# Spreading the weight sums of a down product over two earlier stages, and four small moves in linear attention, in a one-core Trainium2 kernel

## The chip, the cores and the metric

The kernel runs on one core of one Trainium2 chip, as one program. The metric is the time of one execution in microseconds (us) on the device. Before the change three runs took 1881.84, 1878.85 and 1880.43 us, a median of 1880.43 us.

The engines are called as the profile calls them: PE (TensorE, the matmuls; PEld its weight loads), DVE (VectorE), ACT (ScalarE), POOL (GpSimd) and SP (SyncE, which only issues transfers here). POOL issues transfers too, on a queue of its own. Each engine works through its instructions in order, and an instruction that waits holds up all behind it on that engine.

## The reference: what is computed

One step of one layer of a streaming encoder, for two groups of requests together (1024 + 32 rows; the kernel keeps them as 1056 columns, features along the partitions):

```python
h = rms_norm(x, g_pre_mix)
qa, ka, va, ra, alr, qb, kb, vb, ga, gb = split_cols(h @ w_in)
oa, s_gla = gla_branch(qa, ka, va, ra, alr, w_a2, b_a2, g_gla, gla_s0, gla_block)
ob, k_rows, v_rows = attn_fn(qb, kb, vb, rel_bias)
mix = (jax.nn.sigmoid(ga) * (oa @ w_br_a) + jax.nn.sigmoid(gb) * (ob @ w_br_b)) @ w_out
x = x + rms_norm(mix, g_post_mix)
f, conv_new = conv_ffn(rms_norm(x, g_pre_ffn), conv_s0, w_up, conv_w, conv_b, w_down)
x = x + rms_norm(f, g_post_ffn)
gate = jax.nn.sigmoid(rms_norm(x, g_pre_ple) @ w_ple_gate)
x = x + rms_norm(gate * (pe @ w_ple), g_post_ple)
```

`gla_branch` is linear attention with a gate (4 heads, in blocks of rows, with a state carried from block to block), `attn_fn` is softmax attention in a band (8 heads), and `conv_ffn` is an up product (1024 to 2 x 2816), a short causal convolution, a gelu and a down product (2816 to 1024). All of it is float32.

## The kernel before, in words

**Products.** Every fp32 weight is split into a high half `whi` (a copy by ACT) and a low half `wlo` (weight minus high half, by DVE); inputs likewise. A product is then three matmuls: high by high, high by low, low by high. The large products use a Strassen-Winograd scheme: of the eight quarter products of a 2 x 2 partition only seven are formed, from sums of the quarters of the weight and of the input. So weight sums have to be made before such a product begins.

**Stages**, in us from the start of the profiled execution: norm and preparations (0 to 80), the first part of the in product (to 290), attention in a band (to about 560), linear attention (564 to 860), the branch products (to 980), the out product (to 1075), part of the up product ahead of its sums (to 1170), the rest of the up product (to 1540), the down product (to 1770), and the last gate with its norm (to 1875.9). The matmuls that are left of the in product, for the merge gates `ga` and `gb`, are filler: `piece` (L900) issues one small piece of them, and both attentions call it wherever PE would else wait.

**The gate tiles.** A piece on a tile called `Item` ends, after two pieces, in a tile `fv`, written by two ACT copies (L867) from PSUM, and `into` (L745) stores this tile to its places in DRAM (`d_ga`, `d_gb`). Some places are written plainly, others are added to. There are 56 such tiles and 72 stores, 32 plain and 40 that accumulate. All 72 go out on POOL's queue (L748). There are four buffers of `fv`. A tile's weights are split ahead: the high half by ACT (L814, L817), and the low half by DVE (L815, L818), which is put on a list, `fill["lows"]`, that the next `piece` carries out (`lows`, L794). Evacuations of PSUM are put on a list too, `fill["done"]`, and are carried out by `flush` or, all but the last, by `tidy`.

**Weight sums for the down product.** `weight_sum(i, m, at)` (L1152) makes one of sixteen sums of quarters of `w_down`, in DRAM, with three transfers on POOL's queue. It writes one element of its destination `d_ws[i, m]` from a tile that was just computed (L1154; here called the marker, which ties the sum to this place in the program); it copies one quarter there, 704 KB from DRAM to DRAM (L1155); and it adds the second quarter with an accumulating transfer (L1132). The last step goes through the list `later` in `second_sum`, and comes two sums later. The copy waits for the marker, the accumulating transfer for the copy. `branch_sum` (L1134, markers L1138, copies L1139) does the same for the branch product's weights, in sixteen smaller sums of 256 KB each into `d_wa`, during the band. The sums with i = 1 and 3 take `d_ws[0]` and `d_ws[1]` as their first term. The sixteen calls of `weight_sum` stand in `up_strassen(f)` (L2587), one in each f from 0 to 15; f = 16 and 17 call the last two accumulating transfers.

**The band.** Its loop (L1263 on) has nine steps j for each of eight heads g, two heads to a pair hp. `prepare` of the next head fills parts of its tile `bias` on POOL (L976, L977). `band_sums` fills `sums` on POOL (L1162). `branch_sum` stands at j = 1, 4 and 7 of the heads from g = 1 on. VectorE's row sums come at L1035 to L1042.

**Linear attention.** It has sixteen units u = (head h, block s). Each forms scores at several levels: products in PSUM (`one`), copied under masks by DVE into `scores` (`score_copies`, L1470 to L1478), turned by PE (`score_turn`, L1444) and copied back by ACT (`turned`, L1445). Exponentials for the next unit run on ACT (L1364 to L1377). The roots for the norm are L1561 to L1566. `gate_sigmoid` (L834, L835) takes the sigmoids of four gate tiles during u = 15, in two halves each. `slot` (L1652) issues filler pieces; `turn_back` is handed to `level_products` and runs in the middle of the unit. After MAIN pieces the filler is the band's branch product (L890), whose evacuation multiplies by the gates (L844).

**The up product.** `up_strassen(f)` runs for f = 0 to 21. It loads two weight tiles on SP's queue, `raw` and `sraw` (L2497), forms weight sums `ws` on DVE (L2504), and multiplies (L2521 to L2523). For sixteen of the f, the list AHEAD, two of the seven products were made before and stand in DRAM (`d_e`), from where `p1` (L2531) and the first half of `av` (L2582) are loaded on SP's queue. L2580 adds the product of `s2` into the second half of `av`, L2586 forms `q`, whose first element is the marker of the weight sum, and outputs go from `av` and `sm` to `d_b` on POOL's queue (L2364). `av` has three buffers, `sm` one, `raw` and `sraw` two each.

**What sets the order.** In most stages the order on PE, DVE and ACT is the order of the code (a manual schedule); the order on POOL and SP, and on every engine in `up_strassen`, is set by a list scheduler when the program is built.

Of the kernel before, what the change touches and what calls it, by code (L numbers as in the profile page):

```python
# [114 lines left out]
def emit(tc, a):  # L115
# [629 lines left out]
    def into(acc, *places):  # L745
        def store(t):
            for d, h in places:
                po.dma_start(d[:, h], t, **({"accum_op": ALU.add} if acc else {}))  # L748
        return store

    class Item:
# [40 lines left out]
    def lows():  # L792
        for f in fill["lows"]:
            f()  # L794
        fill["lows"].clear()
# [43 lines left out]
    def gate_sigmoid(n):  # L839
        sigmoid(GB[n], GB[n], n)  # L840
# [56 lines left out]
                    yield  # L897
        yield

    def piece():  # L900
        if fill["now"] is None:
            if fill["at"] == len(units):
                return
            fill["now"] = unit_parts(*units[fill["at"]]), 0
        tidy()
        lows()
        parts, n = fill["now"]
        next(parts)
        i, c = units[fill["at"]]
        item = isinstance(tiles[i], Item)  # L910
        fill["now"] = (parts, n + 1) if n < 2 and not item else None
        if n == 0 and fill["split"] == i + 1 <= FIRST and (c in (0, 2) if item else c < 2):
            split_half(int(c > 0))
            if c:
                fill["lows"].append(load_tile)
        if fill["now"] is None:
            fill["at"] += 1
        fill["n"] += 1
        if fill["n"] in PLACES:
            place(*PLACES[fill["n"]])  # L920
# [336 lines left out]
    for i in range(len(WORK) + SK + 1):  # L1257
        g, j = divmod(i, NW)
        hp, hd = divmod(g, 2)
        if g < 8:  # L1260
            if j == 0:
                if hd == 0:
                    band_sums(hp)  # L1263
                steps = prepare(g + 1) if g < 7 else decays(0)
            if j == 3 and hd == 0:
                B[hp]["ob"] = evt()
            WORK[i][0]()
            if SK <= i:
                WORK[i - SK][1]()
            B[hp]["exp"].pop()()  # L1270
            next(steps, None)
            if j % 3 == 2:
                next(made, None)
            if hd == 0 and hp < 3 and j in (5, 7) or hd and hp < 3 and j == 0:
                band_row(hp + 1, {5: 0, 7: 1, 0: 2}[j])
            if g == 7 and j in (6, 7):
                head_value(0, j - 6)
            if j % 3 == 1 and g:
                n = 3 * (g - 1) + j // 3
                if n < 4 * HK:  # L1280
                    branch_sum(n, B[hp]["sums"][hd][0:1, 0:1])
# [317 lines left out]
    flush()  # L1599
    differences(0, range(1, 6))  # L1600
    piece()
    exponentials(0, (7, 6))
    flush()
    piece()
    exponentials(0, (1, 2, 3))
# [43 lines left out]

    SKIP = (5, 8)  # L1650

    def slot(k=1):  # L1652
        for i in range(k):
            slots[0] += 1
            if OB.get("h") is not None or fill["n"] < MAIN and slots[0] % 9 not in SKIP:
                piece()

    level_start(0)
    for u in range(16):
# [29 lines left out]
        def turn_back():  # L1689
            if u == 15:  # L1690
                slot(2)
            if u:
                output_turns(u - 1)
            slot(1)

        level_products(u, (states, turn_back))
        flush()
        if u < 15:
            exponentials(u + 1, (1, 2, 3, 4))
            flush()  # L1700
        score_copies(u, range(4, 7))
        slot(1)
        score_turn(u)
# [8 lines left out]
            results(u - 1)  # L1712
        if u == 15:
            gates(u)
            gate_sigmoid(2)
            gate_sigmoid(3)
            branch_split(1)
        if u < 15:
            factors(u + 1, (7,))
# [44 lines left out]
                OB[x] = tl(bo, [P, 4, T], F32R, tag="b" + x)  # L1764
        if u == 15:
            log_exp()
        roots(u)
        if u == 14:
            branch_split(0)
# [724 lines left out]
    def up_strassen(f):  # L2494
# [89 lines left out]
        Z_ = Z[:, :, :HC]  # L2584
        mul(Z, weight(s1, WL_ENG[2]), "t1", True, True)
        ve.tensor_tensor(q, p1, Z_, op=ALU.add)  # L2586
        if f < 16:  # L2587
            weight_sum(*divmod(f, 4), q[0:1, 0, 0:1])
        elif f < 18:
            second_sum()  # L2590
        if not ahead:
            mul(X, weight(a12, WL_ENG[3]), "b21", False, True)
# [705 lines left out]
```

## Time and profile before

| | |
|---|---|
| median of three runs | 1880.43 us (1878.85 to 1881.84) |
| the profiled execution's own time | 1877.64 us |
| its span in the trace | 1875.9 us |
| mean granted clock of TensorE | 0.994 of full speed |
| busy: ACT, POOL | 1004.4 us (54%), 370.7 us (20%) |
| DMA, POOL's own queue | 161.90 MB, 33.7% of 16 engines' span |
| DMA, SP's and the other hardware queues' | 244.34 MB, 39.2% |
| bytes moved by all queues | 413.24 MB, mean 220 GB/s |

The profile is of one execution, and its span is 1.7 us less than that execution's own time. Busy times count matmuls, copies and the like, on POOL also the issue of transfers. A row of the waits names the waiting group (engine, tile, line), what released it, and then the total us, the number of waits and the longest. In a timeline a row has its start, its duration, the engine and line, and in brackets the idle time before it and what ended it; SPq is SP's queue. The "granted clock" is the share of full speed that TensorE was given.

### The profile page before, as it was taken

The numbers are of one execution on the slowest core, as the hardware profiler recorded it, in microseconds if no ns is written. First come the engines' busy times: TensorE is split into PE (matmuls) and PEld (weight loads), VectorE is DVE, ScalarE is ACT, GpSimd is POOL, SyncE is SP. The second block draws the span as 40 slices with busy tenths as digits, with TensorE's granted clock in tenths as the row PEclk, the third lists the DMA queues.
The fourth block names the chain that finished last, engine by engine and source line by source line (L and its number), as shares of the span: only waits on it lengthen the run. The fifth ranks groups of instructions, "written<-read, shape, count | busy, mean of one in ns | idle before, by whom it ended". The sixth has DMA issues, their size and how long they took to land.

```text
span 1875.9 us, 36253 instructions
## 1 busy us (share of the span) xinstructions
PE 1828.2 (97%) x14000; PEld 1790.9 (95%) x14000; DVE 1298.5 (69%) x2451; ACT 1004.4 (54%) x2126; POOL 370.7 (20%) x641
## 2 busy tenths in 40 slices
PE   9999999999999999999999999999999999999997
PEld 8999998999998998999999999999998999999996
DVE  6955543666656777787756867888876875558776
ACT  7544234666667687675545555333332345555555
POOL 0043341131102231110000121222233211000112
PEclk9999999999999999999999999999999999999999
DMA  7278987567537899887584576789898679987746
GB/s 289 78 230 239 274 215 231 155 189 196 143 113 252 249 255 253 207 222 262 157 272 157 169 274 258 236 249 284 241 250 235 164 204 306 279 285 244 235 150 111
DMA packets 169402, 413.24 MB, mean 220 GB/s; under 512 B 21956, under 2 KB 56972, under 8 KB 168332
## 3 DMA queue, kind: packets, MB, share of 16 engines
q1 hardware_dynamic: 111548, 244.34, 39.2%
q0 software_dynamic: 56240, 161.90, 33.7%
q10 hardware_dynamic: 1440, 4.69, 0.6%
q8 instruction: 110, 1.80, 0.4%
q14 instruction: 64, 0.52, 0.1%
HBM read 270.68 MB, written 181.97 MB: 241 GB/s over the span
## 4 chain that ended last, share of the span: by engine, by line
PE 78%; DMA 6%; DVE 6%; ACT 5%; issue 4%; POOL 1%; SPq 0%; DVEq 0%; ACTq 0%; POOLq 0%
PE two L2521 5%; PE two L2523 5%; PE two L2522 5%; PE two L641 4%; PE two L642 4%; PE two L643 4%; PE two L2970 3%; PE mm L228 3%; PE mm L226 3%; PE two L2972 3%; PE two L2971 3%; PE mm L227 3%; PE mm L890 3%; PE mm L892 2%; PE mm L891 2%
## 5 line engine op out<-in xcount | busy, mean ns | idle before, releaser
L2972 PE MATMUL two<-d,wlo 128*128 128x264 f32 x616 | 174.3, 283 | 0.8 <-DVE wlo L2706 0.8
L2971 PE MATMUL two<-d,whi 128*128 128x264 f32 x616 | 174.7, 284 | 0.2 <-DVE d L2657 0.2
L2970 PE MATMUL two<-d,whi 128*128 128x264 f32 x616 | 174.6, 284 | 0.0
L859 PE MATMUL mm<-xh,whi 128*128 128x264 f32 x448 | 135.2, 302 | 3.6 <-ACT fv L867 3.5
L2511 ACT ACTIVATE whi<-ws 128x512 fp32r<-128x512 f32 x88 | 55.5, 632 | 155.1 <-PE two L2522 147.0
L860 PE MATMUL mm<-xl,whi 128*128 128x264 f32 x448 | 127.4, 284 | 0.0
L861 PE MATMUL mm<-xh,wlo 128*128 128x264 f32 x448 | 127.2, 284 | 0.0
L2522 PE MATMUL two<-ml,whi 128*128 128x264 f32 x448 | 126.5, 283 | 0.0
L2523 PE MATMUL two<-mh,wlo 128*128 128x264 f32 x448 | 126.0, 284 | 0.0
L2521 PE MATMUL two<-mh,whi 128*128 128x264 f32 x448 | 125.8, 283 | 0.0
L2972 PEld LDWEIGHTS two<-d,wlo 128*128 128x128 f32 x616 | 116.4, 189 | 1.1 <-DVE wlo L2706 1.0
L2971 PEld LDWEIGHTS two<-d,whi 128*128 128x128 f32 x616 | 115.8, 188 | 0.4 <-DVE d L2657 0.4
L2970 PEld LDWEIGHTS two<-d,whi 128*128 128x128 f32 x616 | 115.7, 188 | 0.0
L890 PE MATMUL mm<-xh,whi 128*128 128x352 f32 x312 | 108.6, 348 | 1.0 <-ACT fv L734 1.0
L892 PE MATMUL mm<-xh,wlo 128*128 128x352 f32 x312 | 100.9, 324 | 0.0
L891 PE MATMUL mm<-xl,whi 128*128 128x352 f32 x312 | 100.7, 323 | 0.0
L642 PE MATMUL two<-tl,whi 128*128 128x264 f32 x320 | 90.7, 284 | 0.0
L641 PE MATMUL two<-th,whi 128*128 128x264 f32 x320 | 90.7, 284 | 0.0
L643 PE MATMUL two<-th,wlo 128*128 128x264 f32 x320 | 90.7, 284 | 0.0
L859 PEld LDWEIGHTS mm<-xh,whi 128*128 128x128 f32 x448 | 85.0, 190 | 5.5 <-ACT fv L867 4.9
L2706 DVE TENSOR_TENSOR wlo<-wraw,whi 128x512 fp32r<-128x512 f32 (+1 forms) x81 | 51.7, 643 | 49.7 <-ACT whi L2705 49.5
L860 PEld LDWEIGHTS mm<-xl,whi 128*128 128x128 f32 x448 | 84.6, 189 | 0.0
(801 smaller groups left out, 6891.0 us busy)
## 6 DMA issues: line engine op xcount, KB each, us to landing
raw<-in_w_in SPq DMA_DIRECT2D x36, 512.0 KB, 4.8
d_b<-av POOLq DMA_DIRECT2D x33, 528.0 KB, 8.0
d_ws<-in_w_down POOLq DMA_DIRECT2D x24, 704.0 KB, 7.5
uraw<-d_b SPq DMA_DIRECT2D x32, 528.0 KB, 6.3
raw<-in_w_up SPq DMA_DIRECT2D x29, 512.0 KB, 4.9
d_gs<-in_w_in POOLq DMA_DIRECT2D x48, 256.0 KB, 5.5
sraw<-in_w_up SPq DMA_DIRECT2D x22, 512.0 KB, 7.7
wraw<-d_ws SPq DMA_DIRECT2D x16, 704.0 KB, 6.3
```

Source lines behind the costliest of these rows:

```text
L641: pe.matmul(ps[:, j, :HC], w[0][:, k], x[0](k, s), start=st, stop=False, skip_group_check=True)
L642: pe.matmul(ps[:, j, :HC], w[0][:, k], x[1](k, s), start=False, stop=False, skip_group_check=True)
L643: pe.matmul(ps[:, j, :HC], w[1][:, k], x[0](k, s), start=False, stop=sp_, skip_group_check=True)
L859: pe.matmul(ps, h[:, k], xh[:, b, s], start=(k == 0 and not (half and x.chain)), stop=False, skip_group_check=True)
L860: pe.matmul(ps, h[:, k], xl[:, b, s], start=False, stop=False, skip_group_check=True)
L890: pe.matmul(ps, wh, h[:, k, s], start=(k == 0), stop=False)
L2521: pe.matmul(ps[:, j, :HC], w[0][:, k], x[0][:, k, s], start=st, stop=False, skip_group_check=True)
L2522: pe.matmul(ps[:, j, :HC], w[0][:, k], x[1][:, k, s], start=False, stop=False, skip_group_check=True)
L2523: pe.matmul(ps[:, j, :HC], w[1][:, k], x[0][:, k, s], start=False, stop=sp_, skip_group_check=True)
L2970: pe.matmul(o, wh, xh_[:, s], start=(k == 0 and p in (0, 4, 5)), stop=False, skip_group_check=True)
L2971: pe.matmul(o, wh, xl_[:, s], start=False, stop=False, skip_group_check=True)
L2972: pe.matmul(o, wl, xh_[:, s], start=False, stop=(k == HD - 1 and p in (3, 4, 6)), skip_group_check=True)
```

## The change: what it does

It has six edits in the code; the amount of arithmetic and the matmuls stay the same. The order on PE is unchanged, instruction for instruction.

1. **Plain contributions.** `into` issues its 32 plain stores on SP's queue; the 40 accumulating ones stay on POOL's.
2. **Weight sums.** Seven of the sixteen, numbers 0 to 6, now stand in the band, at j = 5 of the heads g = 1 to 7, with the marker taken from `sums`. The other nine stand in the up product in f = 0, 2, 4, ... 16, and f = 19 and 20 call the last two accumulating transfers.
3. **Low halves.** `piece` and `slot` get a parameter `low`. In `turn_back` of all units but the last, the piece doesn't carry out the waiting low halves; the next piece does.
4. **First unit of linear attention.** A `flush` is put between the exponentials of level 7 and those of level 6.
5. **Sigmoids.** Gates 2 and 3 of u = 15 have their sigmoids ahead of `score_copies`, not behind `gates(u)`.
6. **Evacuations in u = 15.** A `flush` follows `log_exp`, ahead of `roots`.

```diff
     def into(acc, *places):
         def store(t):
             for d, h in places:
-                po.dma_start(d[:, h], t, **({"accum_op": ALU.add} if acc else {}))
+                if acc:
+                    po.dma_start(d[:, h], t, accum_op=ALU.add)
+                else:
+                    dma.dma_start(d[:, h], t)
...
-    def piece():
+    def piece(low=True):
...
         tidy()
-        lows()
+        if low:
+            lows()
...
             if g == 7 and j in (6, 7):
                 head_value(0, j - 6)
+            if j == 5 and g:
+                weight_sum(*divmod(g - 1, 4), B[hp]["sums"][hd][0:1, 0:1])
...
-    exponentials(0, (7, 6))
+    exponentials(0, (7,))
+    flush()
+    exponentials(0, (6,))
     flush()
...
-    def slot(k=1):
+    def slot(k=1, low=True):
...
-                piece()
+                piece(low)
...
-            slot(1)
+            slot(1, u == 15)
 
         level_products(u, (states, turn_back))
         flush()
         if u < 15:
             exponentials(u + 1, (1, 2, 3, 4))
             flush()
+        else:
+            gate_sigmoid(2)
+            gate_sigmoid(3)
         score_copies(u, range(4, 7))
...
             gates(u)
-            gate_sigmoid(2)
-            gate_sigmoid(3)
             branch_split(1)
...
         if u == 15:
             log_exp()
+            flush()
         roots(u)
...
-        if f < 16:
-            weight_sum(*divmod(f, 4), q[0:1, 0, 0:1])
-        elif f < 18:
+        if f < 18 and not f % 2:
+            weight_sum(*divmod(7 + f // 2, 4), q[0:1, 0, 0:1])
+        elif f in (19, 20):
             second_sum()
```

In all, POOL has 32 instructions fewer (the plain stores) and SP 32 more; the other engines have as many as before. The instructions of the program after the change stand 3 to 10 lines further down in its code.

**POOL in the up product, at f = 13 and 14.** In these rows d_ws is the destination of the weight sums, in_w_down the weight, c the tile `q` of `up_strassen` (c_2565 that of f = 13, c_2589 that of f = 14), av and sm hold outputs (av_16885 that of f = 12), and gx and convo belong to the convolution. A trailing x2 is a repetition. Before:

```order
L1132 DMA d_ws_3386<-in_w_down 128x1408
L2333 MEMSET gx_17502 128x2
L2334 COPY gx_17502<-convst_83 128x2
L1154 DMA d_ws_3386<-c_2565_17133 1x1
L1155 DMA d_ws_3386<-d_ws_3386 16x11264
L2364 DMA d_b_13342<-av_16885 128x2x528 x2
L2349 COPY convo_84<-gx_17128 128x2
L2350 COPY convo_84<-gx_17128 128x2
L2364 DMA d_b_13342<-sm_17119 128x528
L1132 DMA d_ws_3386<-in_w_down 128x1408
```

The same place after the change (av_16888 is the output of f = 12, sm_17122 the tile that is stored next):

```order
L1136 DMA d_ws_3386<-in_w_down 128x1408
L2343 MEMSET gx_17502 128x2
L2344 COPY gx_17502<-convst_83 128x2
L2374 DMA d_b_13363<-av_16888 128x2x528 x2
L2359 COPY convo_84<-gx_17131 128x2
L2360 COPY convo_84<-gx_17131 128x2
L2374 DMA d_b_13363<-sm_17122 128x528
L2343 MEMSET gx_17686 128x2
L2344 COPY gx_17686<-convst_83 128x2
L1158 DMA d_ws_3386<-c_2589_17320 1x1
```

The marker and the copy of f = 13 are gone from in front of the store of f = 12's output; so is the accumulating transfer behind the store of sm. The marker of f = 14 is still there.

**POOL in the band, in the middle of a head.** Here d_wa is the destination of the branch product's sums with in_w_br_a its weight, sums the tile that the markers are taken from, and bias the next head's tile. Before:

```order
L1138 DMA d_wa_3385<-sums_5238 1x1 x3
L1139 DMA d_wa_3385<-d_wa_3385 128x512 x3
L1132 DMA d_wa_3385<-in_w_br_a 128x512 x2
L1162 MEMSET sums_6053 128x9
L1162 MEMSET sums_6054 128x9
L1132 DMA d_wa_3385<-in_w_br_a 128x512
L976 MEMSET bias_5678 64x64
```

The same head after the change:

```order
L1142 DMA d_wa_3385<-sums_5247 1x1 x2
L1158 DMA d_ws_3386<-sums_5247 1x1
L1142 DMA d_wa_3385<-sums_5247 1x1
L1143 DMA d_wa_3385<-d_wa_3385 128x512 x2
L1159 DMA d_ws_3386<-in_w_down 128x1408
L1143 DMA d_wa_3385<-d_wa_3385 128x512
L1136 DMA d_wa_3385<-in_w_br_a 128x512
L1166 MEMSET sums_6068 128x9
L1166 MEMSET sums_6069 128x9
L1136 DMA d_wa_3385<-in_w_br_a 128x512
L1136 DMA d_ws_3386<-in_w_down 128x1408
L1136 DMA d_wa_3385<-in_w_br_a 128x512
```

The three transfers of one weight sum now stand among the nine of three branch sums; the marker and the copy come ahead of the fills of `sums`, the accumulating transfer comes behind them and ahead of the next fill of `bias`.

**DVE in a unit of linear attention that has a gate piece in `turn_back`.** one is PSUM with the scores of the levels, and wlo a low half of the gate's weights. Before:

```order
L1478 COPY_PREDICATED scores_1147_6950<-masks_3378,one_9497 128x2x8x8
L815 SCALAR_TENSOR_TENSOR wlo_9603<-raw_9428,whi_9602 128x512
L1478 COPY_PREDICATED scores_1147_6950<-masks_3378,one_9498 128x2x4x16
L1478 COPY_PREDICATED scores_1147_6950<-masks_3378,one_9498 128x2x2x32
L1478 COPY_PREDICATED scores_1147_6950<-masks_3378,one_9498 128x2x64
```

After:

```order
L1484 COPY_PREDICATED scores_1147_6971<-masks_3378,one_9518 128x2x8x8
L1484 COPY_PREDICATED scores_1147_6971<-masks_3378,one_9519 128x2x4x16
L1484 COPY_PREDICATED scores_1147_6971<-masks_3378,one_9519 128x2x2x32
L1484 COPY_PREDICATED scores_1147_6971<-masks_3378,one_9519 128x2x64
L818 SCALAR_TENSOR_TENSOR wlo_9624<-raw_9449,whi_9623 128x512
```

The low half has moved from between the score copies to behind the last of them. This happens in eight units.

## The prediction, made before the changed kernel ran

> **What bounds the kernel now.** I read the page first, then TensorE's waits, then the waits of the queues behind the longest of them, then the stretches of time around it.
>
> ```profile
> PE 1828.2 (97%) x14000; PEld 1790.9 (95%) x14000; DVE 1298.5 (69%) x2451; ACT 1004.4 (54%) x2126; POOL 370.7 (20%) x641
> ```
>
> TensorE (PE) is the bound nearly everywhere: of the span of 1875.9 us only 47.7 us are not matmul. The change leaves the matmuls and their order as they are, so it can win only what TensorE waits for, and lose only by new waits. These are the waits of TensorE that bear on the change (total us, times, longest):
>
> ```profile
> PE two L2521 <- DVE av L2580: 9.0, 3, 4.7
> PE mm L859 <- ACT fv L867: 3.5, 5, 1.3
> PE two L1035 <- DVE sm L1041: 3.3, 4, 1.1
> PE one L1444 <- DVE scores L1478: 2.5, 5, 1.1
> PE mm L890 <- DVE ev L844: 1.4, 1, 1.4
> ```
>
> The first row is the up product: 9.0 us in three waits. Their true price is in the stretches of 30 us there (columns: busy time and count of PE, PEld, DVE, ACT, POOL; then granted clock, DMA share, GB/s):
>
> ```profile
> 1380.00:1410.00 30.00, 30.00 (x249) 29.98 (x248) 23.55 (x40) 9.68 (x14) 8.85 (x15) 1.00 0.92 232
> 1410.00:1440.00 30.00, 26.60 (x200) 26.42 (x199) 23.49 (x37) 10.97 (x15) 14.84 (x21) 0.89 0.87 226
> 1440.00:1470.00 30.00, 25.25 (x195) 25.08 (x195) 20.30 (x35) 7.26 (x11) 5.69 (x10) 0.94 0.76 200
> ```
>
> An undisturbed stretch has 249 matmuls. The next two have 200 and 195, which is 49 + 54 = 103 short; at 30/249 = 0.1205 us each that is 12.4 us. Two waits lie in them:
>
> ```profile
> 1414.99 0.56 PE L2521 MATMUL two<-t3h,whi 128*128 128x264 f32 x1 [3.40 <-DVE av L2580]
> ...
> 1457.37 0.36 PE L2521 MATMUL two<-t3h,whi 128*128 128x264 f32 x1 [4.75 <-DVE av L2580]
> ```
>
> 3.40 + 4.75 = 8.15 us is waiting; the other 4.2 us is the granted clock, which falls to 0.89 and 0.94 of full behind them. With the third wait (9.0 - 8.15 = 0.85 us) the up product loses 13.2 us.
>
> **What makes these waits.** L2580 is late because VectorE (DVE), in order, stands before it waiting for a weight load, and that load stands behind another on SyncE's queue. Timelines of GpSimd (POOL), SyncE and VectorE in that order:
>
> ```profile
> 1386.45 0.76 POOL L1154 DMA_DIRECT2D d_ws<-c  x1
> 1392.57 0.54 POOL L1155 DMA_DIRECT2D d_ws<-d_ws  x1 [5.36 <-DMA d_ws<-c]
> 1393.09 2.05 POOL L2364 DMA_DIRECT2D d_b<-av  x2
> ```
>
> ```profile
> 1404.90 0.33 SPq L2582 DMA_DIRECT2D av<-d_e  x1
> 1405.32 0.38 SPq L2497 DMA_DIRECT2D sraw<-in_w_up  x1
> ```
>
> ```profile
> 1411.60 0.69 DVE L2504 TENSOR_TENSOR ws<-sraw 128x512 f32<-128x512 f32 x1 [2.81 <-DMA sraw<-in_w_up]
> ...
> 1414.15 0.69 DVE L2580 TENSOR_TENSOR av<-p,two 128x528 f32<-128x528 f32 x1
> ```
>
> The weight sum of f = 13 writes its marker (L1154) at 1386.45. GpSimd then waits for it to land until 1392.57, copies 704 KB, and only behind that stores f = 12's output d_b<-av. The tile `av` has three buffers, so the load av<-d_e of f = 15 waits for this store until 1404.90. The load of sraw for f = 16 goes out behind it, VectorE gets it at 1411.60, and f = 15's L2580 comes at 1414.15. The groups of waits on GpSimd and SyncE say that this is the rule there:
>
> ```profile
> POOL d_ws L1155 <- DMA d_ws<-c: 77.4, 14, 7.6
> POOL d_ws L1132 <- DMA d_ws<-in_w_down: 26.3, 7, 5.4
> POOL d_ws L1132 <- DMA d_ws<-d_ws: 23.1, 6, 5.5
> ...
> SPq L2582 <- DMA d_b<-av: 46.7, 8, 11.3
> ```
>
> A weight sum costs GpSimd (77.4 + 26.3 + 23.1) / 16 = 7.9 us of waiting, in every f from 0 to 15.
>
> **Weight sums: what is taken away.** Seven of sixteen go to the band, nine stay, in f = 0, 2, ... 16; the accumulates follow their copies as before. For f = 15 what is gone is the marker and copy of f = 13 between f = 12's accumulate and f = 12's store: the store goes out about 1393.1 - 1386.5 = 6.6 us earlier and has no copy ahead of it, so av<-d_e and sraw follow at least 6.6 us earlier, against a wait of 3.40 us. For f = 17 the sum of f = 15 goes: 7.9 us of GpSimd and two transfers, against 4.75 us. The next thing that would then be late is the store behind f = 14's accumulate. So the two large waits should go, and the clock stays at 1.00. As I cannot see the new landings, I keep one wait of the smallest size, 0.85 us: **-12.4 us**; bounds 0 and -13.2.
>
> [...]
>
> **Weight sums: what the band gets.** Each head of the band gains a marker, a copy and an accumulate. The landings (KB each, median us) in the up product and the band's own DMA load:
>
> ```profile
> d_ws<-in_w_down POOLq DMA_DIRECT2D x23, 704.0 KB, 7.5
> d_ws<-d_ws POOLq DMA_DIRECT2D x8, 704.0 KB, 5.8
> ```
>
> ```profile
> 446.01 1.28 POOL L1132 DMA_DIRECT2D d_wa<-in_w_br_a  x1
> 469.58 0.15 POOL L976 MEMSET bias<- 64x64 f32 x1 [22.29 <-DMA bias<-in_rel]
> ```
>
> ```profile
> 500.00:530.00 30.00, 29.46 (x209) 28.15 (x207) 19.77 (x49) 20.27 (x48) 3.29 (x7) 1.00 0.48 135
> ```
>
> GpSimd sits idle 22.29 us at the end of such a head; a sum lands in about 7.5 + 7.5 = 15 us and holds GpSimd 7.9 us, so it fits. Behind it in GpSimd's order stand the fills of `sums` and `bias` and, in the last head, the load for the decays. What hides it is this idle time and a DMA share of 0.48 where the up product has 0.92. Today's waits of the band (L1035, 3.3 us in all) follow VectorE's own row sums, no DMA. I charge **+0.5 us**; bounds 0 and the doubling of that row, +3.3.
>
> **Low halves.** In eight of the sixteen units of linear attention a low half stands between the score copies:
>
> ```profile
> 761.44 0.69 DVE L815 SCALAR_TENSOR_TENSOR wlo<-raw,whi 128x512 fp32r<-128x512 f32 x1
> 762.05 0.95 DVE L1478 COPY_PREDICATED scores<-masks,one 128x128 f32<-128x128 uint8 x3
> ```
>
> Behind the copies it delays the scores no more: 762.05 - 761.44 = 0.61 us sooner, which caps each of the five waits of L1444 (2.5 us in all, the longest 1.1): at most 2.5 - (1.1 - 0.6) = 2.0 us, at least 0, since TensorE may wait next for the copy of `turned`. I take **-1.5 us**. The low half itself is needed an item later; its weight load follows it by those 0.9 us.
>
> **Evacuations.** At the start, the copy `fv` ran behind four exponentials, and TensorE 1.28 us behind it:
>
> ```profile
> 572.02 1.05 ACT L1371 ACTIVATE x<-both,refs 128x64 f32<-128x64 f32 x4
> 572.98 0.36 ACT L867 ACTIVATE fv<-mm 128x264 f32<-128x264 f32 x1
> ```
>
> It comes 0.96 us earlier, but the exponentials of unit 0 come 0.36 us later and end the same preparation: bounds 0 and -1.0, taken **-0.4 us**. At the end, one `ev<-mm` moves ahead of three small operations that wait for ScalarE:
>
> ```profile
> 855.78 0.16 DVE L1564 SCALAR_TENSOR_TENSOR sums<-y,sums 128x3 f32<-128x3 f32 x1 [1.09 <-ACT y L1562]
> ...
> 856.25 0.94 DVE L844 TENSOR_TENSOR ev<-mm,ev 128x352 f32<-128x352 f32 x2
> ```
>
> VectorE is free at 855.78 - 1.09 = 854.7, 1.5 us before 856.25, so the 1.4 us of L890 go but for a rest: **-1.3 us** (0 to -1.4).
>
> **Sigmoids.** Four halves (0.53 us apart) move ahead of `turned`, into ScalarE's idle time there:
>
> ```profile
> 846.03 0.28 ACT L1445 ACTIVATE turned<-one 128x128 f32<-128x128 f32 x1 [2.28 <-PE one L1444]
> 846.21 0.64 ACT L834 ACTIVATE ev<-ev 128x528 f32<-128x528 f32 x1
> 846.74 0.64 ACT L835 ACTIVATE ev<-ev 128x528 f32<-128x528 f32 x1
> ```
>
> 4 x 0.53 = 2.1 us fit into 2.28 us: **0**. If the scores come earlier, `turned` waits for the last sigmoid, up to +0.6 us.
>
> **Plain contributions on SyncE.** 32 stores of `fv` leave GpSimd's queue for SyncE's, where each waits for its copy, with weight loads of linear attention queued behind. What SyncE waits for there, and the copies that need the four `fv` tiles:
>
> ```profile
> SPq L1538 <- DMA d_oa<-sr: 65.0, 15, 9.6
> ```
>
> ```profile
> L867 ACT ACTIVATE fv<-mm x112: 363/389/459, 564.0 to 834.5; 128x264 f32<-128x264 f32 x112
> ```
>
> Two copies fill a tile, so 56 tiles in 270.5 us, one in 4.8 us, and four last 19 us. A store held 9.6 us has some 9 us left to land: **0**, with +3 us (the 3.5 us of L859 again) as the far end.
>
> **The sum** is made against the profiled execution's own time, 1877.64 us (span 1875.9): -12.4 + 0.5 - 1.5 - 0.4 - 1.3 = -15.1, so 1862.5. The median of the runs shown, 1880.43, lies 2.8 above that execution; on it the forecast is **1865.3 us**. Best ends: -13.2 - 2.0 - 1.0 - 1.4 = -17.6, which is 1862.8 on the median; if the 2.8 us are such waits too and go with them, 1860.0.
>
> **Rivals.** (1) *The chain stays half as long.* Sums remain in f = 14 and 16, next to the long run of f = 13 to 15. For it: SyncE waits 46.7 us for these stores, in eight places. Against: sixteen f have a sum today, and TensorE waits in three. Half of 13.2 stays: 1880.4 - 6.6 - 2.7 = 1871.1. Chance 0.12.
> (2) *The up product is short of DMA throughput, not of order*, and its own loads keep the waits. Against: 1380 to 1410 runs at a share of 0.92 without a wait, and the 4.75 us fall where the share is 0.76. Then only the band's charge and linear attention count: 1880.4 + 0.5 - 3.2 = 1877.7, no change. [...] Chance 0.07.
> (3) *SyncE holds up linear attention:* stores that wait for `fv` delay the weight loads. About 1 us in each of the eight units with plain stores: 1865.3 + 8 = 1873. For: SyncE's 65.0 us; against: the 9 us to spare. Chance 0.06.
> (4) *Slower: the band breaks.* GpSimd blocks so long on markers and copies that the bias fill (L976) of the next head comes late, then L1041, then L1035. It decides where a sum holds GpSimd over 22.3 us, not 7.9. At 26 us it costs 3.7 us in each of seven heads: 1865.3 + 26 = 1891. Chance 0.04.
>
> **How the numbers follow.** The forecast has 0.71. About 0.2% (3.8 us) is what a measurement of this kernel can tell from no change: faster is below 1876.7. The forecast, (1) and (3) are faster: 0.71 + 0.12 + 0.06 = 0.89, less 0.01 for a tail of (3); same is (2) and that tail, 0.08; slower is (4), 0.04. The range reaches from 1860.0 to rival (1) with the band's far end and the spread of the runs (1881.84 is 1.4 above their median): 1871.1 + 2.8 + 1.4 = 1875.3. It holds the forecast but for its tails, (1) and (3), about 0.85; (2) and (4) lie outside.
>
> **What would show it.** In the new profile: no wait of L2521 on L2580 over 1 us; stretches of 249 matmuls from 1200 to 1550; a clock of 1.00 there; SyncE's wait for d_b<-av well under 46.7 us; L1444's waits under 1 us in all; no wait of L890 on L844; GpSimd still idle before each bias fill. Wrong if the up product's waits are there with half the sums, or if L1035 waits clearly over 3.3 us.

## The result and the profile after

The changed kernel took 1867.88 us (median of four runs, 1865.28 to 1872.21), the kernel before 1881.13 us beside it (four runs, 1878.85 to 1886.14). The ratio is 0.9928, with a 95% interval from 0.9901 to 0.9956. A second measurement of the same kernel, among the experiments, gave 1865.71 us and a ratio of 0.9905 (0.9884 to 0.9926). The forecast was 1865.3 us, in a range from 1860.0 to 1875.3.

The profiled execution took 1872.21 us, the longest of the four runs, with a span of 1870.5 us. So the two profiles lie only 5.4 us apart, where the medians lie 13.2 us apart, and the profile has to be read by places. The page's first line:

```profile
PE 1826.9 (98%) x14000; PEld 1789.8 (96%) x14000; DVE 1298.1 (69%) x2451; ACT 1005.0 (54%) x2126; POOL 351.9 (19%) x609
```

TensorE has the same 14,000 instructions. Its waits (total us, times, longest), with the rows that answer to those of before:

```profile
PE one L1522 <- DVE turned L1454: 4.2, 1, 4.2
PE mm L893 <- ACT fv L734: 3.4, 1, 3.4
PE two L1039 <- DVE sm L1045: 3.2, 4, 1.0
PE mm L862 <- ACT fv L870: 2.1, 5, 0.8
...
PE mm L893 <- DVE ev L847: 0.4, 1, 0.4
...
PE one L1450 <- DVE scores L1484: 0.3, 1, 0.3
```

The row of 9.0 us, the up product's wait for `av`, has gone altogether. L1444 (now L1450) has 0.3 us left of 2.5, L890 behind L844 (now L893 behind L847) 0.4 of 1.4. But a wait has come that was not there, 4.2 us at L1522, and the wait at the head of the band behind L734 has 3.4 us where it had 1.0. The stretches of 30 us in the up product (columns as before):

```profile
1380.00:1410.00 30.00, 30.00 (x250) 30.00 (x249) 26.74 (x45) 10.95 (x14) 8.50 (x16) 1.00 0.87 229
1410.00:1440.00 30.00, 30.00 (x250) 30.00 (x249) 24.68 (x39) 11.59 (x16) 10.95 (x17) 1.00 0.85 214
1440.00:1470.00 30.00, 30.00 (x250) 30.00 (x249) 26.33 (x43) 11.58 (x15) 5.87 (x13) 1.00 0.92 234
```

All three have 250 matmuls and the full clock, at a DMA share of 0.85 to 0.92. On GpSimd and SyncE (rows of two timelines, and then one of SyncE's waits) one sees why:

```profile
1386.89 0.84 POOL L1136 DMA_DIRECT2D d_ws<-in_w_down  x1 [5.91 <-DMA d_ws<-d_ws]
1391.24 2.02 POOL L2374 DMA_DIRECT2D d_b<-av  x2 [2.47 <-DVE av L2369]
```

```profile
1398.55 0.33 SPq L2541 DMA_DIRECT2D p<-d_e  x1
1401.70 0.33 SPq L2592 DMA_DIRECT2D av<-d_e  x1
1402.32 0.33 SPq L2507 DMA_DIRECT2D sraw<-in_w_up  x1
```

```profile
SPq L2592 <- DMA d_b<-av: 6.1, 3, 2.7
```

The store of f = 12's output waits only for VectorE now, not for a marker, and SyncE's waits for such stores have fallen from 46.7 to 6.1 us.

Since every kernel here has the same 14,000 TensorE instructions in the same order, the start of the n-th can be set side by side in two traces. The time between two such starts is worked out so for each kernel below; the rows after the first are differences from before, in us. No. 2,340 lies at the head of the band, 4,060 to 6,200 is linear attention, 8,500 to 11,000 is the up product.

| kernel | to 2,340 | band to 4,060 | linear attention to 6,200 | to 8,500 | up product to 11,000 | to the end |
|---|---|---|---|---|---|---|
| before | 309.6 | 253.2 | 298.9 | 316.6 | 317.1 | 380.5 |
| after | +6.2 | 0.0 | +0.7 | -0.3 | -13.8 | +1.8 |
| after, second profile | +2.4 | 0.0 | +1.5 | -2.3 | -13.8 | +1.3 |
| spread_only | +5.0 | 0.0 | -1.1 | -1.6 | -13.8 | +0.5 |
| into_only | +1.1 | +1.5 | +0.5 | -2.0 | -1.5 | +1.7 |
| linear_only | +7.0 | 0.0 | +0.5 | -2.8 | -1.0 | -0.2 |
| late_lows_only | +1.7 | -0.1 | +2.6 | -0.7 | +5.2 | -0.2 |
| no_late_lows | +5.3 | +1.6 | +1.9 | -2.1 | -13.8 | +2.0 |
| two_moved | +1.5 | -0.1 | +1.2 | -1.1 | -13.0 | -0.1 |
| bytes_on_act | +2.6 | 0.0 | -3.9 | -2.2 | -13.3 | +1.3 |
| waits_alone | +1.7 | +1.5 | -5.2 | -0.6 | -12.0 | +2.0 |
| place_early | +1.2 | 0.0 | -6.4 | -0.7 | -13.8 | +1.7 |
| place_early_12 | +1.8 | 0.0 | -2.5 | -1.2 | -13.8 | +1.3 |
| bytes_on_sp | +1.8 | +1.5 | -5.1 | -0.2 | +177.5 | +1.6 |

Up to no. 2,340 there is nothing of the change, and all others took 1.1 to 7.0 us longer than the profile of before: that execution had an unusually quick start. Some of the scatter is the clock. The four kernels with +1.5 or +1.6 us in the band each have one stretch of 3.4 us at half clock there, and no other kernel has one; before alone has one in the column to 8,500, from 949.3 to 952.7 us. The gain of the change is in the up product, 13.8 us, the same in every trace with edit 2 whole and nothing added. Linear attention, where three gains were forecast, shows none in the two profiles of the changed kernel.

### The profile page after: what moved, and what is told of

Same layout as the page of the kernel before. It is cut to its first block, busy times and chain, and to the rows that moved or that the text cites. A ratio compares the mean times of both kernels' runs of the same rounds, so it can differ in the third digit from the quotient of the medians.

```text
span 1870.5 us, 36262 instructions
## 1 busy us (share of the span) xinstructions
PE 1826.9 (98%) x14000; PEld 1789.8 (96%) x14000; DVE 1298.1 (69%) x2451; ACT 1005.0 (54%) x2126; POOL 351.9 (19%) x609
## 4 chain that ended last, share of the span: by engine, by line
PE 82%; DMA 6%; DVE 5%; ACT 5%; issue 2%; POOL 0%; SPq 0%; ACTq 0%; DVEq 0%; POOLq 0%
PE two L2533 6%; PE two L2531 6%; PE two L2532 6%; PE mm L228 3%; PE mm L226 3%; PE mm L227 3%; PE two L2980 3%; PE two L2982 3%; PE two L2981 3%; PE two L641 3%; PE two L642 3%; PE two L643 3%; PE mm L893 3%; PE mm L862 3%; PE mm L863 2%; PE mm L895 2%
## 5 line engine op out<-in xcount | busy, mean ns | idle before, releaser
L893 PE MATMUL mm<-xh,whi 128*128 128x352 f32 x312 | 109.6, 351 | 3.4 <-ACT fv L734 3.4
```

The costliest lines, as they stand in the source:

```text
L893: pe.matmul(ps, wh, h[:, k, s], start=(k == 0), stop=False)
```

## The experiments

The theory at the start: the gain is edit 2 (the weight sums), by the order of GpSimd's queue; edits 3 to 6 bring some 3 us. Rivals: the other edits carry it; or the number of bytes moved in the up product does. A second question came from the profile: whose work is the wait of 4.2 us at L1522? Every ratio below is to the kernel before on the same chip.

**spread_only**: the kernel before with edit 2 alone.

```diff
+            if j == 5 and g:
+                weight_sum(*divmod(g - 1, 4), B[hp]["sums"][hd][0:1, 0:1])
...
-        if f < 16:
-            weight_sum(*divmod(f, 4), q[0:1, 0, 0:1])
-        elif f < 18:
+        if f < 18 and not f % 2:
+            weight_sum(*divmod(7 + f // 2, 4), q[0:1, 0, 0:1])
+        elif f in (19, 20):
```

> The kernel before with edit 2 alone: seven weight sums in the band, nine in every second f of the up product. Theory (order on GpSimd's queue): this is nearly all of the gain, about -13 us against before (the matmuls of both traces, set side by side, put -13.6 us on the up product), no wait of L2521 on L2580 over 1 us, and nothing lost in the band. Rival (the other edits carry a good part): less than half of it, -6 us or less.

Measured: 1865.24 us, ratio 0.9906 (0.9883 to 0.9929): as much as the whole change. The up product is 13.8 us shorter, the band costs 0.0, and the waits elsewhere (L1446 is L1444) are as before:

```profile
PE two L1035 <- DVE sm L1041: 3.3, 4, 1.1
PE mm L859 <- ACT fv L867: 3.2, 5, 1.3
...
PE one L1446 <- DVE scores L1480: 2.1, 5, 0.7
```

So edit 2 carries the gain, and beside it the other edits show no further gain in the median of the changed kernel; the intervals would hide some 3 us. (Without edit 2 the up product's loss differs between executions: the three kernels below that lack it lie at -1.5, -1.0 and +5.2 us beside the profile of before.)

**linear_only**: the kernel before with edits 3 to 6.

```diff
-    exponentials(0, (7, 6))
+    exponentials(0, (7,))
+    flush()
+    exponentials(0, (6,))
...
-            slot(1)
+            slot(1, u == 15)
...
+        else:
+            gate_sigmoid(2)
+            gate_sigmoid(3)
...
         if u == 15:
             log_exp()
+            flush()
```

> The kernel before with edits 3 to 6 alone (low halves, exponentials, sigmoids, evacuations in linear attention). Theory: -2 to -3.5 us, the waits of L1444 and the 1.4 us of L890 gone, the up product's 9 us of L2521 on L2580 still there. Rival (the late low halves hold the gate weights' buffers, so that the load raw<-d_gs comes late, and the 4.25 us wait of L1522 in the profile after is the change's own work): that wait of about 4 us is seen here too, at the same matmul, and the time is the same as before or above.

Measured: 1878.30 us, ratio 0.9979 (0.9960 to 0.9999). The wait is there at the same matmul:

```profile
739.10 1.22 PE L1517 MATMUL one<-vt,turned 128*128 128x256 f32 x2 [4.58 <-DVE turned L1449]
```

In this profile linear attention is 0.5 us longer than before: what the edits win is spent on this wait and what follows it (in the kernel after, where the wait ends at 738.43 us, the granted clock is 0.50 from 737.3 to 744.1). The wait spoke for the rival, with edit 3 as its cause. The time did not: the median of twelve runs is 4.0 us under before, with an interval that just excludes no change, and the profiled run, with 1881.00 us, lies above that median. The next runs test edit 3.

**into_only**: the kernel before with edit 1.

```diff
+                if acc:
+                    po.dma_start(d[:, h], t, accum_op=ALU.add)
+                else:
+                    dma.dma_start(d[:, h], t)
```

> The kernel before with edit 1 alone: 32 plain stores on SyncE's queue. Theory: no difference, within 1 us, and no new wait of TensorE in linear attention. Rival (SyncE holds up the weight loads behind the stores): +3 us or more, with waits of L859 or L1516 on loads of raw.

Measured: 1885.05 us, ratio 1.0005 (0.9988 to 1.0023), no difference. Linear attention is 0.5 us longer, and neither of the rival's waits shows.

**after_again**: the kernel after, unchanged.

> The kernel after, unchanged, for a second profile. Theory (the two waits that the first profile has beyond before, 3.45 us at the start of the band and 4.25 us at L1522, are scatter between executions): neither comes back over 2 us, and the time is 0.7% under before. Rival (they belong to the change): both, or the one at L1522, come back at the same matmul with 3 to 5 us.

Measured: 1865.71 us, ratio 0.9905 (0.9884 to 0.9926). The wait at L1522 came back with 3.9 us, the one at the head of the band with 2.3. The theory that both were scatter did not hold for L1522.

**no_late_lows**: the kernel after without edit 3.

```diff
-            slot(1, u == 15)
+            slot(1)
```

> The kernel after without edit 3 (the low halves run where they ran before; edits 1, 2 and 4 to 6 stay). Theory (edit 3 makes the weight loads of linear attention later, and so the wait of 3.9 to 4.6 us at L1522 that the three profiles with edit 3 show and the three without it don't): that wait is gone, L1444 waits some 2 us again, and the time is 2 to 4 us under the kernel after (about 0.9885 of before). Rival (edits 4 to 6 cause the wait): it is there still, with about 4 us, and the time is 2 us above the kernel after, the gain of the low halves being lost.

Measured: 1866.09 us, ratio 0.9933 (0.9910 to 0.9955). The wait is still there, so edit 3 is not needed for it:

```profile
PE one L1522 <- DVE turned L1454: 4.2, 1, 4.2
...
PE one L1450 <- DVE scores L1484: 1.6, 5, 0.7
```

**late_lows_only**: the kernel before with edit 3 alone.

```diff
-    def piece():
+    def piece(low=True):
...
-        lows()
+        if low:
+            lows()
...
-            slot(1)
+            slot(1, u == 15)
```

> The kernel before with edit 3 alone. Theory: the wait at L1522 is there (3.9 to 4.6 us, and the lower clock behind it some 2.4 us more), the waits of L1444 fall under 0.6 us, and linear attention is 1.5 to 3 us longer than before. Rival (edits 4 to 6 cause the wait): no wait there, and linear attention 2 to 3 us shorter.

Measured: 1880.45 us, ratio 0.9993 (0.9974 to 1.0012), the wait with 4.1 us, linear attention 2.6 us longer. So it comes with edit 3 alone, and with edits 4 to 6 (and 1 and 2) alone. My theory for it fell; the loads tell more. In the profile of the kernel after, rows of GpSimd, SyncE, ScalarE and TensorE:

```profile
725.98 0.99 POOL L778 DMA_DIRECT2D xl<-d_t  x1
```

```profile
716.11 0.42 SPq L1599 DMA_DIRECT2D d_oa<-sr  x1
723.11 0.37 SPq L1544 DMA_DIRECT2D sr<-d_sr  x1
723.57 0.42 SPq L1529 DMA_DIRECT2D out_o_gs<-ss  x1
727.30 0.35 SPq L1539 DMA_DIRECT2D ss<-in_state_gla  x1
727.75 0.87 SPq L790 DMA_DIRECT2D raw<-d_gs  x2
```

```profile
737.25 0.63 ACT L820 ACTIVATE whi<-raw 128x512 fp32r<-128x512 f32 x1 [5.83 <-DMA raw<-d_gs]
737.78 0.26 ACT L1451 ACTIVATE turned<-one 128x128 f32<-128x128 f32 x1
```

```profile
738.43 0.79 PE L1522 MATMUL one<-vt,turned 128*128 128x256 f32 x1 [4.25 <-DVE turned L1454]
```

ScalarE's copy of `turned` stands behind the high half of a gate weight, and that waits for its load `raw`, which went out 1.8 us behind a 1 MB load of `xl` and took 9.5 us. SyncE was late because sr<-d_sr waits there for the store d_oa<-sr to land, which went out 7.0 us before it, and `ss` waits 3.2 us for the store out_o_gs. In spread_only, where nothing waits, GpSimd, SyncE and ScalarE have:

```profile
727.14 0.79 POOL L775 DMA_DIRECT2D xl<-d_t  x1 [0.50 <-DMA xl<-fv]
```

```profile
727.14 0.94 SPq L787 DMA_DIRECT2D raw<-d_gs  x2
```

```profile
731.68 0.62 ACT L817 ACTIVATE whi<-raw 128x512 fp32r<-128x512 f32 x1
```

Both loads go out together, and ScalarE takes `raw` 4.5 us later. In the kernel after, `xl` lands at 736.98 and `raw` 0.24 us behind it, at 737.22; in spread_only `raw` lands at 730.94 and `xl` at 737.63. Of the twelve traces with the two loads in these places, counting the runs below, five have `raw` 1.8 to 2.0 us behind `xl`: its landing takes 8.9 to 9.6 us there, comes 0.2 to 1.2 us after that of `xl`, and TensorE waits 3.9 to 4.6. Seven have it no more than 0.02 us behind, and no wait. A load of `raw` is 128 packets of 2048 bytes. If the first 128 such packets behind the issue are taken as its own, they end 2.7 to 3.5 us before the landing in the five, and 0.3 to 1.8 in the six of the seven whose landing the trace has; so some 3 of the 9 us come behind the last of these packets. The packets also begin later, 3.4 to 4.2 us after the issue against 1.1 to 2.2. That the load of `xl` holds up that of `raw` is my reading of these traces; in what way it would, no run shows.

**two_moved**: the kernel before with the sums of f = 13 and 15 alone taken out.

```diff
+            if j == 5 and g in (1, 2):
+                weight_sum(0, g - 1, B[hp]["sums"][hd][0:1, 0:1])
...
-        if f < 16:
-            weight_sum(*divmod(f, 4), q[0:1, 0, 0:1])
-        elif f < 18:
+        if f < 16 and f not in (13, 15):
+            weight_sum(*divmod(2 + f - (f > 13), 4), q[0:1, 0, 0:1])
+        elif f in (16, 17):
```

> The kernel before, with the weight sums of f = 13 and 15 alone taken out of the up product (two sums more in the band; the other fourteen stay in f = 0 to 12 and 14). Theory (the two large waits come from the marker and copy that stand ahead of the store of the output of f = 12 and of f = 14): both are gone or under 1 us, and the up product is 9 to 12 us shorter than before. Rival (what counts is how much is moved through GpSimd's queue over the whole stage): less than a third of the gain, the waits come elsewhere, -1 to -4 us.

Measured: 1869.77 us, ratio 0.9945 (0.9924 to 0.9967); the up product is 13.0 us shorter. Two sums of sixteen bring nearly all of it, although SyncE still waits for stores in nine places, all but 0.4 us of it within the slack (rows of SyncE's waits and of TensorE's):

```profile
SPq L2584 <- DMA d_b<-av: 31.2, 9, 6.7
```

```profile
PE two L2523 <- DVE av L2582: 0.4, 1, 0.4
```

**bytes_on_sp**: the kernel after with extra copies on SyncE's queue.

```diff
+        if 3 <= f < 16 and f % 2:
+            for i in range(3):
+                dma.dma_start(d_dm[f // 2, i], d_b[0:5:4, f - 3] if f < 14 else d_b[5:7, f - 14])
```

> The kernel after, with three extra copies of 541 KB from DRAM to DRAM in each f = 3, 5, ... 15, on SyncE's queue, into a place that nothing reads: more bytes in the up product than the seven sums that were moved away brought, with no marker and nothing in GpSimd's queue. Theory (order, not throughput): no wait of L2521 on L2580 comes back over 1 us, and the time is within 3 us of the kernel after. Rival (throughput): the waits come back, and the up product loses 8 us or more.

Measured: 2059.02 us, ratio 1.0946 (1.0922 to 1.0970). The waits came back in all seven places, with 22 to 29 us each (rows of TensorE's and of VectorE's waits, then two stretches):

```profile
PE two L2532 <- DVE av L2591: 174.3, 7, 28.5
```

```profile
DVE ws L2515 <- DMA sraw<-in_w_up: 197.1, 7, 32.2
```

```profile
1200.00:1230.00 30.00, 16.11 (x133) 15.90 (x132) 9.03 (x16) 3.63 (x5) 3.80 (x8) 0.83 0.43 155
1230.00:1260.00 30.00, 18.62 (x131) 18.65 (x132) 19.36 (x30) 8.72 (x12) 4.69 (x9) 0.71 0.49 142
```

But the DMA share is 0.43 and 0.49 in these stretches, not 0.9: the 16 engines together were not short of time. VectorE waited seven times, 197.1 us in all, for the load of `sraw`, which stood behind these copies on their own queue. Why the three copies of a place, 1.6 MB, took so long at so low a share was not shown. The rival's signs came, but by way of this queue and not of a high share, and the run tells nothing on throughput. (The 541 KB are 540,672 bytes, 528 KB as the profile counts the 704 KB.) The next one changes queue and shape.

**bytes_on_act**: the kernel after with the same bytes in the same seven places (f = 3, 5, ... 15), now on ScalarE's queue, where no load of the up product stands behind them, each copy in 256 rows of 2112 bytes.

```diff
+        if 3 <= f < 16 and f % 2:
+            o = d_b[0:5:4, f - 3] if f < 14 else d_b[5:7, f - 14]
+            for i in range(3):
+                ac.dma_start(d_dm[f // 2, i], o.rearrange("q p t -> p q t"))
```

> [...] Theory (order, not throughput): waits of L2521 on L2580 stay under 3 us in all, and the time is within 4 us of the kernel after. Rival (throughput): the waits come back in most of the seven places, and the up product loses 8 us or more.

Measured: 1862.44 us, ratio 0.9892 (0.9873 to 0.9910). The up product loses 0.5 us against the kernel after. Two of its stretches:

```profile
1200.00:1230.00 30.00, 30.00 (x248) 29.86 (x247) 27.01 (x44) 11.74 (x16) 8.00 (x15) 1.00 0.87 285
1380.00:1410.00 30.00, 30.00 (x248) 29.80 (x247) 26.35 (x44) 9.95 (x14) 9.27 (x15) 1.00 1.00 281
```

Even at a DMA share of 1.00 TensorE doesn't wait. From 1170 to 1540 us the queues moved 90.8 MB here, before the change 85.9 and after it 78.9. That rules out the rival of throughput, as far as plain copies can stand for accumulating ones.

**waits_alone**: the kernel after with the markers and transfers of the odd f, but of 64 bytes.

```diff
+        if f < 16 and f % 2:
+            po.dma_start(d_dm[f // 2, 0:1, 0:1], q[0:1, 0, 0:1])
+            po.dma_start(d_dm[f // 2], quarter_of(0, 0)[0][0:1, 0:16])
+            second_sum(d_dm[f // 2], quarter_of(1, 0)[0][0:1, 0:16])
```

> The kernel after, with a marker, a copy and an accumulating transfer of 64 bytes each in every f = 1, 3, ... 15, into a place that nothing reads: the order and the waits on GpSimd's queue as before the change, without the bytes. Theory in its strong form (GpSimd's waits for markers alone make the stores late): waits of L2521 on L2580 come back, 3 us or more in all. Weaker form (it takes the marker's long landing behind queued sums, 6.3 us, and the copy ahead of the store): the tiny transfers land in some 2 to 4 us, the waits stay under 1 us, and the time is that of the kernel after.

Measured: 1867.09 us, ratio 0.9905 (0.9889 to 0.9921). Rows of GpSimd's, SyncE's and TensorE's waits:

```profile
POOL d_dm L2604 <- DMA d_dm<-c: 36.8, 8, 6.2
```

```profile
SPq L2593 <- DMA d_b<-av: 32.1, 8, 10.3
```

```profile
PE two L2532 <- DVE av L2591: 1.5, 1, 1.5
```

The order alone, with hardly a byte, brings SyncE's wait for the stores from 6.1 back to 32.1 us; before it was 46.7. Nearly all of that is within TensorE's slack: one wait of 1.5 us returns, and the up product is 1.8 us longer than after. Counted from the start of no. 8,500, the two loads of `av` that the large waits hung on go out at 226.7 and 262.3 us before, at 216.9 and 245.0 after, and at 219.3 and 254.3 here. So the waits alone bring back a quarter and a half of the lateness, and 1.8 of the 13.8 us. Neither form of the theory fits whole: the wait is under the 3 us of the strong one, but a marker with nothing large behind it still held GpSimd 36.8 / 8 = 4.6 us, not 2 to 4, among the nine sums that are left. For the full loss it takes the 704 KB transfers on GpSimd's queue as well; copy and accumulating transfer were not told apart.

**place_early**: the kernel after with the last load of `xl` three filler pieces earlier.

```diff
-(60, Q12, "t4", 0), (66, Q12, "t4", 1))}
+(60, Q12, "t4", 0), (63, Q12, "t4", 1))}
```

> The kernel after, with one 1 MB load xl<-d_t (the last of the eight that change the input's quarters in linear attention) three filler pieces earlier; the list scheduler then also sets the next weight load raw<-d_gs ahead of sr<-d_sr on SyncE's queue. Theory (the wait at L1522 is there where raw is issued behind xl<-d_t and lands 8 to 9 us later, and not there where it goes first; ten traces agree): raw lands before it is needed, the wait of 3.9 to 4.6 us and the lower clock behind it are gone, and the time is 4 to 7 us under the kernel after, about 0.987 of before. Rival (the wait is an accident of these executions and no part of the median): the profile may lack it, but the time is that of the kernel after within 2 us.

Measured: 1861.30 us (1859.62 to 1863.52), ratio 0.9878 (0.9860 to 0.9896), the lowest of all. GpSimd, SyncE and ScalarE there:

```profile
712.82 0.80 POOL L778 DMA_DIRECT2D xl<-d_t  x1 [5.41 <-DMA xl<-fv]
```

```profile
715.56 0.82 SPq L790 DMA_DIRECT2D raw<-d_gs  x2
716.48 0.49 SPq L1544 DMA_DIRECT2D sr<-d_sr  x1
```

```profile
725.84 0.62 ACT L820 ACTIVATE whi<-raw 128x512 fp32r<-128x512 f32 x1
```

`raw` still goes out 2.7 us behind `xl`, but 10.3 us before ScalarE takes it, and the wait is gone. So it is not the order of the two loads alone that makes the wait, as the theory had it, but also how late both are. Two things are changed here at once, the place of the load of `xl` and, through the scheduler, that of `raw` ahead of sr<-d_sr; which of them is enough was not tried. Linear attention is 6.4 us shorter than before.

**place_early_12**: the same with edits 1 and 2 only.

> The kernel before with edits 1 and 2 and the load xl<-d_t three pieces earlier, without edits 3 to 6. It measures edits 3 to 6 with the wait at L1522 out of the way in both: beside the kernel with all edits and the early load (0.9878 of before). Theory (edits 3 to 6 are worth 4 to 5 us where that wait doesn't come; it comes in part of the executions with them): no wait at L1522 here either, linear attention 4 to 6 us longer than with them, about 0.990 of before. Rival (they are worth nothing, and the early load brought the gain): 0.988.

Measured: 1864.57 us, ratio 0.9915 (0.9890 to 0.9939), no wait at the place of L1522, linear attention 2.5 us shorter than before. Against place_early, edits 3 to 6 are worth 6.4 - 2.5 = 3.9 us in the traces and 1864.57 - 1861.30 = 3.3 us in the medians (of two measurements, whose intervals overlap). Both are rough: without edits 3 to 6 and without the early load linear attention lies from -1.1 to +1.2 us beside before. The early load by itself shows no gain: this kernel has 0.9915, spread_only, which lacks it and edit 1, 0.9906.

## Why the prediction was right, and where it was not

**Right in sum, and for its main reason.** The time is within 2.6 us of the forecast, and the largest term, the up product, has the cause that was given: spread_only shows that edit 2 does it, two_moved that the sums of f = 13 and 15 do nearly all of it, bytes_on_act that throughput doesn't, waits_alone that the waits on GpSimd's queue make the stores late, though they cost little without the 704 KB transfers. The up product was taken at -12.4 and measured -13.8, past the bound of -13.2: the third wait that I kept went too, and the clock stayed whole. From no. 10,300 to 11,000, where the two large waits lay, the matmuls of after take 12.6 us less; 12.6 - 8.15 = 4.4 us of that is the clock, near the 4.2 counted. Two stretches of before show it:

```profile
1412.00:1422.00 10.00, 7.01 (x38) 7.04 (x39) 8.70 (x15) 4.04 (x5) 3.91 (x8) 0.66 0.90 219
1452.00:1462.00 10.00, 5.25 (x31) 5.08 (x30) 9.47 (x14) 3.40 (x4) 0.31 (x3) 0.83 0.36 110
```

The clock is 1.00 or 0.50 there, so a mean of 0.66 and 0.83 over 10 us is 6.8 us at half, from 1413.5 on, and 3.4 us, from 1457.9 on. Of the 6.8 the first 1.5 fell into the wait itself, which ended at 1414.99, so (6.8 - 1.5 + 3.4) / 2 = 4.4.

That the sum came so near is in part luck: the up product gave 1.4 us more than counted, and in the two profiles after linear attention gave 3.9 to 4.7 us less than its three gains.

**Rival (1), half of the chain,** is out: no wait is left. **Rival (2), throughput,** is out by bytes_on_act. **Rival (4), the band,** is out: 0.0 us in most traces against a charge of +0.5, and the +1.5 us of some is the stretch at half clock, which into_only has without any moved sum. That is in spite of a DMA share that rose from 0.48 to 0.60 from 500 to 530 us:

```profile
500.00:530.00 30.00, 29.68 (x211) 28.55 (x210) 19.15 (x47) 20.29 (x50) 4.07 (x8) 1.00 0.60 162
```

GpSimd's idle time before the fill of the bias, 22.29 us in the head shown, is 19.08 us in the same head now:

```profile
475.88 0.15 POOL L980 MEMSET bias<- 64x64 f32 x1 [19.08 <-DMA bias<-in_rel]
```

**Low halves, evacuations, sigmoids.** The three gains summed to -3.2 us. Where the wait at L1522 doesn't come, the pair of place_early runs has -3.9. The row of L1444 went from 2.5 to 0.3 us, and without edit 3 it is 1.6, so in this pair the low halves bring 1.3 of the 1.5 foreseen. The row scatters: over all traces it is 1.6 to 2.8 us without edit 3 and 0.3 to 1.3 with it. The evacuation at the end brought 1.0 of 1.3. The one at the start was undersized: the wait of 1.28 us is 0.33 now, so it took 0.95 where I had 0.4; the later exponentials of unit 0 cost nothing.

**The step that failed** is that linear attention was costed by its own waits alone: "its weight load follows it by those 0.9 us" was written, and nothing charged for a weight load that comes later. With the wait at L1522 linear attention won nothing: +0.7 and +1.5 us in the two profiles after. It costs 3.9 to 4.6 us of waiting, and the low clock behind it some 2.4 more (in the first of the two 8.9 us late at L1522, 11.3 us twenty matmuls on, both against before). Rival (3) had named late weight loads as the danger, but from the stores on SyncE, which into_only shows to cost nothing, and as a loss in eight small pieces.

**What stays open.** What decides whether `raw` goes out ahead of `xl` was not settled. In the five traces with the wait the store d_oa<-sr took longer to land, 6.5 to 7.7 us against 4.0 to 5.6 in the others that have its landing, and so held SyncE. All five kernels have edits 3 to 6 or a part of them, and none of the four without them shows the wait; but bytes_on_act, waits_alone and bytes_on_sp have all of these edits, with the same linear attention as the kernel after, and do not show it. So the same instructions of linear attention go either way in different kernels. These three alone also declare a new tile in DRAM, `d_dm`, ahead of `d_oa`; whether the place of `d_oa` matters, or chance decides, was not tried, and the one kernel that was profiled twice had the wait both times. That the edits make the wait more frequent is likely from 5 of 8 against 0 of 4, and not shown. That it was in the median of the changed kernel is an inference from the time of place_early, some 4 us under it.

## What to carry to other kernels

A wait of the bound engine may be made three queues away: here a tiny marker on GpSimd's queue (5.36 us of waiting in the place shown before the change) delayed a store, the store a load on SyncE, the load a sum on VectorE, for which TensorE waited 3.40 us. Look for what stands ahead of a store on an in-order queue, and take away what meets the slowest step, before moving everything: two of sixteen sums were worth 13.0 of 13.8 us. When small waits are removed in a stage whose loads go out just in time, check which large load the next small one will fall behind; with edits 3 to 6 in, moving the large load earlier went with a ratio of 0.9878 against 0.9905 and 0.9928, and without them with no gain.

## What the runs showed of the hardware that was not expected

- Three copies of 541 KB from DRAM to DRAM with an outermost dimension of 2, on the queue of the loads, made TensorE wait 22 to 29 us, at a DMA share of 0.43 and 0.49 in the two stretches shown. As many bytes in copies of 256 rows, on another queue, cost some 0.5 us in the whole stage. Queue and shape were changed together, so their parts are not told apart.
- A marker of 4 bytes held GpSimd 77.4 / 14 = 5.5 us on the mean before the change. After it, with nine of the sixteen sums, it was 21.6 / 9 = 2.4 us:

```profile
POOL d_ws L1159 <- DMA d_ws<-c: 21.6, 9, 3.6
```

- In the five traces where the load of `raw` (256 KB) went out 1.8 to 2.0 us behind the 1 MB load of `xl` on another queue, it landed in 8.9 to 9.6 us, just behind it; where it went out with it or ahead, it landed in 3.4 to 6.1 us.
- The clock fell behind a wait of under 2 us, and not each time. Before has a wait of 1.89 us that ends at 948.3 us, and half clock from 949.3 to 952.7; the same wait of 1.8 us in the kernel after has none. In into_only and waits_alone half clock follows two waits of 1.7 us in all early in the band, from 330.9 and 331.6 us on, and in before and after the same two waits go without.
